# The gate and up biases of 32 experts: rows spread by GpSimd and added by VectorE in place of bias matmuls

## The chip, the cores and the metric

The kernel runs on one core of one Trainium2 chip. The metric is the device time of one execution in microseconds (us). Before the change the median of three runs is 2063.8 us (2061.73 to 2067.09).

## What is computed

One layer of an encoder: a mixer, cross-attention and a mixture of experts over 1024 tokens of width 1024, all in float32. The change lies in the experts. Each token goes to 4 of 32 experts; an expert multiplies its tokens by a gate/up matrix of 1024x2048, adds a bias of 2048, puts the halves through a clamped SwiGLU and multiplies by a down matrix of 1024x1024. Cut to that:

```python
def expert_block(args):
    xb, e = args
    gu = xb @ w_gate_up[e] + b_gate_up[e]
    gate = jnp.minimum(gu[:, :D_EXPERT], SWIGLU_LIMIT)
    up = jnp.clip(gu[:, D_EXPERT:], -SWIGLU_LIMIT, SWIGLU_LIMIT)
    glu = gate * jax.nn.sigmoid(SWIGLU_ALPHA * gate)
    return ((up + 1.0) * glu) @ w_down[e] + b_down[e]
```

`SWIGLU_LIMIT` is 7, `SWIGLU_ALPHA` 1.702.

## The kernel before, in words

**Order of the experts.** Up to the first expert the kernel computes the mixer, the attention and the router, and fills a table of slots: which token, with which weight, stands at which place of which expert. Expert 31 (`STATIC`) comes first, since it needs no ranking. The others are ranked by their number of tokens while the first one runs, and the ranking is written to `ordr`, from which the number of each next expert is read (`prologue`, L925). The first 17 ranks (`N32`) have a remainder of up to 32 tokens beyond 128: they are called heavy here. The 14 others have up to 128 tokens: light. `rank_order` mixes heavy and light ones. What exceeds these sizes is left to a loop at the end (`beyond`).

**One expert.** Its weights come in 12 chunks of 1 MB: `j` = 0 to 7 gate and up (two column halves `c`, two halves `g` of the contraction, `t` for gate or up), 8 to 11 down. Float32 is multiplied as a sum of products of rounded parts: each chunk `raw` is split into `eh` by ScalarE (L134) and the rest `el` by VectorE (L135), and `main_mm` (L1038) runs three matmuls for each of its four slices (L1062, L1063, L1064). An expert has 24 places, two per chunk, and the work of the other engines is issued at a place: `glu_main` for half 0 at place 7 and for half 1 at 15, then `h_main` (transposes of `hh`, L1009, and the split into `hthl`), `x_main` of the next expert, and at 23 `y_main`, which scatters the result into `acc_d` by GpSimd. The tables `PLACE_*` say where the transposes stand, `AHEAD_*` how many chunks ahead the splits run at each place. The order of the instructions on each engine is that of the code.

**Remainders.** The up to 32 rows of a heavy expert go through plain float32 matmuls in `rem_mm` (L1085), sixteen per chunk pair, at places that `plan` puts into `agenda`. Their bias is added in `h_rem` from a small tile `bT`, transposed; the change doesn't touch it.

**The bias.** `b_gate_up` has 2048 values per expert. `bias_load` and `bias_table` bring all of it into one tile `BT` before the first expert: gate halves on partitions 0 to 63, up halves on 64 to 127, each as a rounded part (32 partitions) and a rest (32). In `main_mm`, at the first gate chunk of each half, a pair of matmuls (L1049, in a loop over `t`) picks the expert's row by a one-hot column of `ohr` and writes it to all 128 rows of the banks for gate and up; the products of the chunks are summed on top (`start=j >= 8 and ...`). `ohr` comes from the ranking (`ranks`). `glu` then reads the banks: two clamps from PSUM on VectorE (L1000, L1002), the sigmoid on ScalarE (L1001), two products on VectorE (L1003, L1004).

**Queues.** SP issues the loads of the chunks (L973) and of the small index tables `idx` and `idr`; a chunk is asked for when a buffer is free (`load_more`). GpSimd issues the gathers of token rows (L936, `xg` and `xgr`, for the next expert) and the scatters (L940), and the first expert's chunks from the third on. Pool `s8` has 20 tiles of a chunk's size ([128, 2048]), `s4` 7 of [128, 1024], `t2` 6 of [128, 512].

Of the kernel before, what the change touches and what calls it, by code (L numbers as in the profile page):

```python
# [9 lines left out]
F32 = mybir.dt.float32  # L10
F32R = mybir.dt.float32r
# [52 lines left out]
def rem_rows(r):  # L64
    if r < N64 or r == STATIC:
        return 64
    return 32 if r < N32 else 0
# [12 lines left out]
def kernel(ctx: ExitStack, tc: tile.TileContext, A, out, dbg=None):  # L80
    nc = tc.nc
    PS = bass.MemoryType.PSUM
    cp = ctx.enter_context(tc.tile_pool(name="cp", bufs=1))
    dp = ctx.enter_context(tc.tile_pool(name="dp", bufs=1, space=bass.MemoryType.DRAM))
# [7 lines left out]
    def mm_bank(name="mm"):  # L92
        return mmp.tile([P, H2], F32, name=name, tag="mm")
# [7 lines left out]
    def s8(name, shape, dt=F32):  # L101
        return mp.tile(list(shape), dt, name=name, tag="s8", bufs=20)

    def s4(name, shape, dt=F32):
        return mp.tile(list(shape), dt, name=name, tag="s4", bufs=7)

    def t2(name, shape=(P, H2), dt=F32):
        return mp.tile(list(shape), dt, name=name, tag="t2", bufs=6)

    def small(name, shape, dt=F32, bufs=1):  # L110
        return mp.tile(list(shape), dt, name=name, bufs=bufs)
# [5 lines left out]
    def f(ap):  # L117
        return ap.bitcast(F32)
# [81 lines left out]
    acc_d = dp.tile([S + P, D], F32, name="acc_d")  # L200
    h_d = dp.tile([S + P, D], F32, name="h_d")
    x1_d = dp.tile([2, KT, P, H2], F32, name="x1_d")
    tab_d = dp.tile([NE * ESTR, 2], I32, name="tab_d")
    ov_d = dp.tile([NBLK, 2], I32, name="ov_d")
    hs = [slice(h * H2, (h + 1) * H2) for h in range(2)]
# [64 lines left out]
    eid = cp.tile([P, 8], F32, name="eid")  # L270
# [66 lines left out]
    b = sum_cols([sx])  # L337
# [13 lines left out]
    b = sum_cols([sx])  # L351
# [226 lines left out]
    ps = {}  # L578
# [38 lines left out]
    for ft in range(KT):  # L617
        wh, wl = next_w(0)
        for h in range(2):
            xr = t2("xres")  # L620
            nc.sync.dma_start(out=xr, in_=A["xT"][h, ft])
            for g, (yh, yl) in enumerate(((ych, ycl), (yfh, yfl))):
                ps = mm_bank()
# [117 lines left out]
    for fc in range(2):  # L741
        VW.append([(s8(f"vwh{fc}{q}", [P, 4, H2], F32R), s8(f"vwl{fc}{q}", [P, 4, H2], F32R)) for q in range(2)])
        for hd in range(4):
            w = next_w(0)
            for mt in range(2):
                ps = mm_bank()
# [3 lines left out]
                j = hd * 2 + mt  # L750
# [45 lines left out]
    scat = []  # L796
    tiles = [dict() for _ in range(8)]
    lt = {}
    BT = []

    def tile_r(x2):

# [114 lines left out]
    order = rank_order()  # L917
    ready, ex = [False], []
    st = [None] * NE
# [78 lines left out]
    def glu(hdst, pg, pu, n, m, tmp=None):  # L998
        g, sg, u = tmp or (t2("g"), t2("sg"), t2("u"))
        nc.vector.tensor_scalar(g[:m, :n], pg, LIMIT, None, op0=ALU.min)  # L1000
        nc.scalar.activation(sg[:m, :n], g[:m, :n], AF.Sigmoid, scale=ALPHA)  # L1001
        nc.vector.tensor_scalar(u[:m, :n], pu, LIMIT, -LIMIT, op0=ALU.min, op1=ALU.max)  # L1002
        nc.vector.tensor_tensor(g[:m, :n], g[:m, :n], sg[:m, :n], op=ALU.mult)  # L1003
        nc.vector.scalar_tensor_tensor(hdst, u[:m, :n], 1.0, g[:m, :n], op0=ALU.add, op1=ALU.mult)  # L1004
# [33 lines left out]
    def main_mm(i, j, middle=None):  # L1038
        s = st[i]
        c, g, t = (j // 4, (j % 4) // 2, j % 2) if j < 8 else (j % 2, (j - 8) // 2, 0)  # L1040
        key, l = ("gu"[t] + str(c), s["xt"]) if j < 8 else ("d" + str(c), s["ht"])
        if g == 0 and j >= 8:
            s[key] = mm_bank(key)
        elif g == 0 and t == 0:
            r = s["r"]
            for t in range(2):
                tsl = slice(t * 64, t * 64 + 64)
                b = s["gu"[t] + str(c)] = mm_bank(key)
                nc.tensor.matmul(b, ohr[tsl, r:r + 1].to_broadcast([64, P]), BT[0][tsl, hs[c]], start=True, stop=False)  # L1049
        raw, wh, wl = ch[12 * i + j][:3]  # L1050
        ps = s[key]
        if wh is None:
            for k in range(4):
                nc.tensor.matmul(ps, f(l[:, 0, g * 4 + k, :]), raw[:, k, :], start=j >= 8 and g == 0 and k == 0, stop=g == 1 and k == 3)  # L1054
                if k % 2 and steps:
                    steps.pop(0)()
                if k == 1 and middle:
                    middle()
            return
        for k in range(4):  # L1060
            kk = g * 4 + k
            nc.tensor.matmul(ps, l[:, 0, kk, :], wh[:, k, :], start=j >= 8 and g == 0 and k == 0, stop=False)  # L1062
            nc.tensor.matmul(ps, l[:, 0, kk, :], wl[:, k, :], start=False, stop=False)  # L1063
            nc.tensor.matmul(ps, l[:, 1, kk, :], wh[:, k, :], start=False, stop=g == 1 and k == 3)  # L1064
            if k % 2 and steps:
                steps.pop(0)()
            if k == 1 and middle:
                middle()
# [21 lines left out]
    def glu_main(i, c):  # L1090
        s = st[i]
        s[f"h{c}"] = t2("hh")
        glu(s[f"h{c}"], s[f"g{c}"], s[f"u{c}"], H2, P)

    def h_main(i, c):
        s = st[i]
# [8 lines left out]
    def h_rem(i, c):  # L1105
# [15 lines left out]
        nc.vector.tensor_scalar(g, tv[:, :, 0], LIMIT, None, op0=ALU.min)  # L1121
        nc.scalar.activation(sg, g, AF.Sigmoid, scale=ALPHA)
        nc.vector.tensor_scalar(u, tv[:, :, 1], LIMIT, -LIMIT, op0=ALU.min, op1=ALU.max)
# [75 lines left out]
    def plan(i):  # L1199

        lead, lx, lt, l0, l1, ly = REM
        at = lambda p, fn, *arg: agenda.setdefault(p, []).append(lambda: fn(*arg))
# [7 lines left out]
        at(p + 22 + ly, y_rem, i)  # L1210

    agenda = {}
    for i in range(1, NE):
        if rem_rows(order[i]):
            plan(i)


# [8 lines left out]
        ex.append(e)  # L1226

    def bias_load():

        BT.extend([s4("BT", [P, D], F32R), s8("braw", [P, D])])  # L1230
        for i in range(4):
            nc.scalar.dma_start(out=BT[1][i * 32:(i + 1) * 32], in_=A["b_gate_up"][:, (i // 2) * D:(i // 2 + 1) * D])

    def bias_table():
        nc.scalar.activation(BT[0], BT[1], AF.Copy)
        for i in (32, 96):
            nc.vector.tensor_tensor(BT[0][i:i + 32], BT[1][i:i + 32], f(BT[0][i:i + 32]), op=ALU.subtract)

    def x2_chunk(c0, hooks):
        h, cn = c0 // H2, HF  # L1240
# [31 lines left out]
    xA = x2_chunk(0, places([(load_router,)], [(load_bias,)], [(row_table,)], [(padding,)], [(prepare,)], [(prepare_bias,)]))  # L1272
    xB = x2_chunk(HF, places(*two_tiles(0, xA, 0)))
    C = two_tiles(2, xB, HF)
    C[5].append((bias_load,))
    xC = x2_chunk(H2, places(*C))
    prologue(0)
    first = lambda: load_more(RAWS_FIRST)
# [8 lines left out]
        [(tile_s, 5), (tile_e, 5)]))  # L1287
    dump("h", h_d)
    dump("acc", acc_d)
    ohr = small("ohr", [P, NE], F32R)  # L1290
    ordr = small("ordr", [1, NE + 1], I32)

    nc.vector.tensor_copy(ohr[:, STATIC:STATIC + 1], eid[:, 4:5])
    x_main(0, 0)
    tile_r(xD)
    bias_table()
    x_main(0, 1)
    tile_a(6, xD, H2 + HF)
    tile_a(7, xD, H2 + HF)
# [5 lines left out]
    def count_order():  # L1305
        rk = s4("rk", [P, D])
        cnt, key, gt, R = rk[:, 0:4], rk[:, 32:64], rk[:, 64:96], rk[:, 96:128]
# [20 lines left out]
        def ranks():  # L1328
            ps = sm_bank("ordps")
            nc.tensor.matmul(ps[:1, 0:NE], eid[:32, 0:1], R[:32], start=True, stop=True)  # L1330
            nc.vector.tensor_copy(ordr[:, 0:NE], ps[:1, 0:NE])
            nc.vector.tensor_copy(ohr, R)
            ready[0] = True

        ps3 = {}
# [171 lines left out]
    def both(*fs):  # L1507
        def go():
            for g in fs:
# [6 lines left out]
    base, r = fin["base"], fin["r"]  # L1516
# [4 lines left out]
                                 in_=base, in_offset=None)  # L1521
# [84 lines left out]
```

## Time and profile before

| | |
|---|---|
| median of three runs | 2063.8 us (2061.73 to 2067.09) |
| profiled execution, its own time | 2069.46 us |
| its span | 2067.6 us |
| PE busy | 2028.4 us, 98% |
| PE weight loads busy | 1513.3 us, 73% |
| VectorE busy | 1585.7 us, 77% |
| ScalarE busy | 1122.3 us, 54% |
| GpSimd busy | 227.3 us, 11% |
| DMA | 513.26 MB, mean 248 GB/s |

The profile is one execution, taken by the hardware profiler. PE is TensorE's matmuls, PEld its weight loads (they overlap the matmuls), DVE VectorE, ACT ScalarE, POOL GpSimd, SP the engine that issues most loads. An engine's busy time is the union of its instructions. Matmuls are pipelined: the length given for one is longer than the distance from it to the next. "L1064" is line 1064 of the kernel. The granted clock of TensorE over the span was 0.99 of full speed, the higher of its two levels, 2.4 GHz.

### The profile page before, as it was taken

Reading aid. Unit: us, or ns where it says so; the run is one execution under the profiler, and the core shown is the slowest. Engines: PE = TensorE matmul, PEld = TensorE weight load, DVE = VectorE, ACT = ScalarE, POOL = GpSimd, SP = SyncE. Lnnn points to the kernel's source line nnn. Section 1 sums busy time; section 2 is a strip of 40 time slices with the busy share of each in tenths; the row PEclk is TensorE's granted clock in tenths of the full one; section 3 lists DMA queues with packets and bytes.
Section 4 is the critical chain, followed back from the end, with each engine's and each line's share of the span. In section 5 each row is a group of like instructions: output and inputs, shape, how many; then the busy total and the mean of one; then the engine's idle time right before and its main releaser. Section 6 shows DMA issues by size and latency. Waiting matters only on the chain. (4 is left out here: it accounts for less than half of the span.)

```text
span 2067.6 us, 28604 instructions
## 1 busy us (share of the span) xinstructions
PE 2028.4 (98%) x10745; PEld 1513.3 (73%) x10745; DVE 1585.7 (77%) x1991; ACT 1122.3 (54%) x1195; POOL 227.3 (11%) x190
## 2 busy tenths in 40 slices
PE   8999999999999999999999999999999999999996
PEld 6888988888984567677776677676776676776764
DVE  6667668445576788888888798888988788888876
ACT  5233533334213566675666676666666576666754
POOL 0000100000133111010101111010111110110101
PEclk9999999999999999999999999999999999999999
DMA  4112434112358689898897998898998799898976
GB/s 156 47 62 72 133 125 161 31 42 86 107 192 302 231 286 358 302 318 321 310 363 254 333 320 323 306 362 302 318 327 304 283 339 320 306 348 298 332 301 249
DMA packets 104640, 513.26 MB, mean 248 GB/s; under 512 B 21298, under 2 KB 25651, under 8 KB 55347
## 3 DMA queue, kind: packets, MB, share of 16 engines
q1 hardware_dynamic: 83600, 445.87, 57.3%
q0 software_dynamic: 14080, 48.54, 9.4%
q10 hardware_dynamic: 6818, 16.99, 2.3%
q8 instruction: 86, 1.41, 0.3%
q14 instruction: 56, 0.45, 0.1%
HBM read 473.41 MB, written 37.95 MB: 247 GB/s over the span
## 5 line engine op out<-in xcount | busy, mean ns | idle before, releaser
L135 DVE TENSOR_TENSOR el<-raw,eh 128x2048 fp32r<-128x2048 f32 x372 | 831.0, 2287 | 121.3 <-ACT eh L134 119.8
L134 ACT ACTIVATE eh<-raw 128x2048 fp32r<-128x2048 f32 x372 | 690.6, 1908 | 7.1 <-PEq L1402 4.6
L1062 PE MATMUL g<-eh,xthl 128*128 128x512 f32 x992 | 401.2, 404 | 0.0
L1064 PE MATMUL g<-eh,xthl 128*128 128x512 f32 x992 | 388.1, 391 | 2.2 <-issue 2.2
L1063 PE MATMUL g<-el,xthl 128*128 128x512 f32 x992 | 388.5, 392 | 1.3 <-DVE el L135 1.3
L1062 PEld LDWEIGHTS g<-eh,xthl 128*128 128x128 f32 x992 | 186.5, 188 | 79.3 <-issue 39.7
L1064 PEld LDWEIGHTS g<-eh,xthl 128*128 128x128 f32 x992 | 186.6, 188 | 43.6 <-issue 2.6
L1063 PEld LDWEIGHTS g<-el,xthl 128*128 128x128 f32 x992 | 186.8, 188 | 36.9 <-DVE el L135 1.6
L1062 PE MATMUL d<-eh,hthl 128*128 128x512 f32 x496 | 205.9, 415 | 0.0
L1064 PE MATMUL d<-eh,hthl 128*128 128x512 f32 x496 | 195.1, 393 | 0.0
L1063 PE MATMUL d<-el,hthl 128*128 128x512 f32 x496 | 194.0, 391 | 0.0
L1085 PE MATMUL r<-raw,xrt 128*32 128x512 f32 (+1 forms) x1152 | 144.8, 598 | 0.7 <-ACT xrt L1036 0.7
L1001 ACT ACTIVATE sg<-g 128x512 f32<-128x512 f32 x64 | 40.4, 631 | 175.8 <-DVE g L1000 172.3
L940 POOL DMA_INDIRECT acc_d<-y,idx x31 | 74.4, 2400 | 393.1 <-ACT y L1131 296.4
L1062 PEld LDWEIGHTS d<-eh,hthl 128*128 128x128 f32 x496 | 93.2, 188 | 28.1 <-ACT xthl L134 10.9
L1064 PEld LDWEIGHTS d<-eh,hthl 128*128 128x128 f32 x496 | 93.1, 188 | 21.2
L1063 PEld LDWEIGHTS d<-el,hthl 128*128 128x128 f32 x496 | 93.6, 189 | 16.0
L134 ACT ACTIVATE hthl<-tp 128x512 fp32r<-128x512 f32 x62 | 37.1, 599 | 120.5 <-PE tp L1009 120.5
L145 PE MATMUL mm<-xh,wh 128*128 128x512 f32 x232 | 92.2, 397 | 6.0 <-ACT xh L137 6.0
L147 PE MATMUL mm<-xh,wl 128*128 128x512 f32 x232 | 91.0, 392 | 0.5 <-DVE wl L135 0.5
L146 PE MATMUL mm<-xl,wh 128*128 128x512 f32 x232 | 91.2, 393 | 0.0
L135 DVE TENSOR_TENSOR wl<-wraw,wh 128x1024 fp32r<-128x1024 f32 (+1 forms) x57 | 70.3, 1233 | 22.9 <-ACT wh L134 18.9
(377 smaller groups left out, 3243.0 us busy)
## 6 DMA issues: line engine op xcount, KB each, us to landing
raw<-in_w_exp SPq DMA_DIRECT2D x375, 1024.0 KB
raw<-in_w_exp POOLq DMA_DIRECT2D x9, 1024.0 KB
wraw<-in_w_in SPq DMA_DIRECT2D x15, 512.0 KB
xraw<-in_xT SPq DMA_DIRECT2D x16, 256.0 KB
wraw<-in_w_k SPq DMA_DIRECT2D x8, 512.0 KB
wraw<-in_w_v SPq DMA_DIRECT2D x8, 512.0 KB
wraw<-in_w_out SPq DMA_DIRECT2D x8, 512.0 KB
xres<-in_xT SPq DMA_DIRECT2D x16, 256.0 KB
```

What stands on the lines that cost most here:

```text
L134: nc.scalar.activation(dh, src, AF.Copy)
L135: nc.vector.tensor_tensor(dl, src, f(dh), op=ALU.subtract)
L145: nc.tensor.matmul(ps, lh, rh, start=start and i == 0, stop=False)
L146: nc.tensor.matmul(ps, lh, rl, start=False, stop=False)
L147: nc.tensor.matmul(ps, ll, rh, start=False, stop=stop and i == n - 1)
L940: nc.gpsimd.indirect_dma_start(out=dst, out_offset=bass.IndirectOffsetOnAxis(ap=idx, axis=0), in_=src, in_offset=None, compute_op=ALU.add)
L1001: nc.scalar.activation(sg[:m, :n], g[:m, :n], AF.Sigmoid, scale=ALPHA)
L1062: nc.tensor.matmul(ps, l[:, 0, kk, :], wh[:, k, :], start=j >= 8 and g == 0 and k == 0, stop=False)
L1063: nc.tensor.matmul(ps, l[:, 0, kk, :], wl[:, k, :], start=False, stop=False)
L1064: nc.tensor.matmul(ps, l[:, 1, kk, :], wh[:, k, :], start=False, stop=g == 1 and k == 3)
L1085: nc.tensor.matmul(ps[o:o + m], lhs[:, g * 4 + kk, :], ch[12 * i + j - 1 + t][0][:, kk, :], start=k == 0 and g == 0, stop=k == 4 // n - 1 ...
```

## The change

Both halves of the banks are now started by the chunks' own products, and the bias is added when VectorE reads them. For each expert and half, `bias_row` loads one row of 4 KB (512 gate and 512 up values) into partition 0 of a tile `bt` [128, 2, 512] by SP's queue, and `bias_rows` copies partition 0 to all 128 partitions by GpSimd (`partition_broadcast`). `glu_main` reads the banks with an add of `bt`, and no longer uses `glu`. The one of `(up + 1.0)` is added once to the table of biases (`bias_one`), which goes to DRAM as `bias_d`; the clamp of up is from -6 to 8 accordingly. The sigmoid is taken of the unclamped gate and clamped afterwards by its value at 7 (`SIGMOID_LIMIT`). `BIAS` holds the places: the row of half 0 is asked for three places before the expert's start and copied at its place 1, that of half 1 at places 5 and 9; in the first expert the first row comes before `x_main(0, 0)`. `BT`, `ohr`, `bias_table` and the pairs of matmuls are gone. `glu` stays for the loop `beyond`.

```diff
+BIAS = ((-3, 1), (5, 9))
...
-        if g == 0 and j >= 8:
+        if g == 0:
             s[key] = mm_bank(key)
-        elif g == 0 and t == 0:
-            r = s["r"]
-            for t in range(2):
-                tsl = slice(t * 64, t * 64 + 64)
-                b = s["gu"[t] + str(c)] = mm_bank(key)
-                nc.tensor.matmul(b, ohr[tsl, r:r + 1].to_broadcast([64, P]), BT[0][tsl, hs[c]], start=True, stop=False)
...
-            nc.tensor.matmul(ps, l[:, 0, kk, :], wh[:, k, :], start=j >= 8 and g == 0 and k == 0, stop=False)
+            nc.tensor.matmul(ps, l[:, 0, kk, :], wh[:, k, :], start=g == 0 and k == 0, stop=False)
...
         s[f"h{c}"] = t2("hh")
-        glu(s[f"h{c}"], s[f"g{c}"], s[f"u{c}"], H2, P)
+        g, sg, u = t2("g"), t2("sg"), t2("u")
+        bt = s[f"b{c}"]
+        nc.vector.tensor_tensor(g, s[f"g{c}"], bt[:, 0, :], op=ALU.add)
+        nc.scalar.activation(sg, g, AF.Sigmoid, scale=ALPHA)
+        nc.vector.tensor_tensor(u, s[f"u{c}"], bt[:, 1, :], op=ALU.add)
+        nc.vector.tensor_scalar(u, u, LIMIT + 1.0, 1.0 - LIMIT, op0=ALU.min, op1=ALU.max)
+        nc.vector.scalar_tensor_tensor(u, sg, SIGMOID_LIMIT, u, op0=ALU.min, op1=ALU.mult)
+        nc.vector.scalar_tensor_tensor(s[f"h{c}"], g, LIMIT, u, op0=ALU.min, op1=ALU.mult)
+
+    def bias_row(i, c):
+
+        s = st[i]
+        bt = s[f"b{c}"] = s4("bt", [P, 2, H2])
+        nc.sync.dma_start(out=bt[0:1], in_=bias_d[ds(s["e"], 1)].rearrange("o (t c f) -> o t c f", t=2, c=2)[:, :, c, :])
+
+    def bias_rows(i, c):
+        bt = st[i][f"b{c}"]
+        nc.gpsimd.partition_broadcast(bt.rearrange("p t f -> p (t f)"), bt[0:1].rearrange("p t f -> p (t f)"))
...
-    for i in range(1, NE):
-        if rem_rows(order[i]):
+    for i in range(NE):
+        for c, (row, rows) in enumerate(BIAS):
+            if i or c:
+                agenda.setdefault(24 * i + row, []).append(lambda i=i, c=c: bias_row(i, c))
+            agenda.setdefault(24 * i + max(rows, 0 if i else 1), []).append(lambda i=i, c=c: bias_rows(i, c))
+        if i and rem_rows(order[i]):
             plan(i)
...
-    def bias_table():
-        nc.scalar.activation(BT[0], BT[1], AF.Copy)
-        for i in (32, 96):
-            nc.vector.tensor_tensor(BT[0][i:i + 32], BT[1][i:i + 32], f(BT[0][i:i + 32]), op=ALU.subtract)
+        bb.append(s8("braw", [NE, 2 * D]))
+        nc.scalar.dma_start(out=bb[0], in_=A["b_gate_up"])
+
+    def bias_one():
+
+        nc.vector.tensor_scalar(bb[0][:, D:], bb[0][:, D:], 1.0, None, op0=ALU.add)
+        nc.scalar.dma_start(out=bias_d[:, :], in_=bb[0])
```

**GpSimd, a light expert and the heavy one behind it.** The rows are the engine's instructions in their order; `acc_d<-y` is the scatter of an expert's result, `xg` and `xgr` are gathers for the next expert, `acc_d<-yr` scatters a remainder. Before:

```order
L940 DMA acc_d<-y,idx 1152x1024
L936 DMA xg<-h_d,idx 128x1024
L936 DMA xgr<-h_d,idr 32x1024
L940 DMA acc_d<-y,idx 1152x1024
L936 DMA xg<-h_d,idx 128x1024
L940 DMA acc_d<-yr,ids 2304x512
L940 DMA acc_d<-y,idx 1152x1024
```

Now, with the lines of the changed kernel:

```order
L943 DMA acc_d<-y,idx 1152x1024
L1107 ISA bt<-bt 128x1024
L939 DMA xg<-h_d,idx 128x1024
L939 DMA xgr<-h_d,idr 32x1024
L1107 ISA bt<-bt 128x1024
L943 DMA acc_d<-y,idx 1152x1024
L1107 ISA bt<-bt 128x1024 x2
L939 DMA xg<-h_d,idx 128x1024
L943 DMA acc_d<-yr,ids 2304x512
L943 DMA acc_d<-y,idx 1152x1024
```

In the light expert the first copy stands behind the scatter of the expert before and ahead of both gathers, the second behind the gathers; in the heavy expert both copies stand between the scatter and the gather `xg`.

**GpSimd, the first expert.** `tab_d` is the table of slots, `rk` a scratch tile of the ranking, `raw` the first expert's chunks. Before:

```order
L901 DMA tab_d<-pl,slot 36864x2
L906 MEMSET spacer 1x4
L1312 IOTA rk 32x64
L936 DMA xgr<-h_d,idr 64x1024
L973 DMA raw<-in_w_exp 128x2048 x3
```

Now:

```order
L904 DMA tab_d<-pl,slot 36864x2
L909 MEMSET spacer 1x4
L1327 ISA
L1327 IOTA rk 32x64
L1107 ISA
L1107 ISA bt<-bt 128x1024
L939 DMA xgr<-h_d,idr 64x1024
L976 DMA raw<-in_w_exp 128x2048 x3
```

Three instructions came between the scatters into the table and the gather `xgr`: a copy, and two rows without tiles, one ahead of the iota and one ahead of the copy. Two more such rows stand ahead of the program's first copy (L1107) and ahead of the last tensor_tensors (L1507).

**VectorE, the second half of a light expert's products.** `el` is the rest of a chunk's split, `g_...` and `u_...` are the banks in PSUM. Before:

```order
L135 TENSOR_TENSOR el<-raw,eh 128x2048 x6
L1000 TENSOR_SCALAR g<-g_7759 128x512
L1002 TENSOR_SCALAR u<-g_7761 128x512
L1003 TENSOR_TENSOR g<-g,sg 128x512
L1004 SCALAR_TENSOR_TENSOR hh<-u,g 128x512
L135 TENSOR_TENSOR el<-raw,eh 128x2048 x2
L135 TENSOR_TENSOR hthl<-tp,hthl 128x512
```

Now:

```order
L137 TENSOR_TENSOR el<-raw,eh 128x2048 x6
L1092 TENSOR_TENSOR g<-g_7774,bt 128x512
L1094 TENSOR_TENSOR u<-u_7794,bt 128x512
L1095 TENSOR_SCALAR u<-u 128x512
L1096 SCALAR_TENSOR_TENSOR u<-sg,u 128x512
L1097 SCALAR_TENSOR_TENSOR hh<-g,u 128x512
L137 TENSOR_TENSOR el<-raw,eh 128x2048 x2
L137 TENSOR_TENSOR hthl<-tp,hthl 128x512
```

Four operations between the splits became five; the splits stand as before. On TensorE nothing moved but the 128 bias matmuls, which are gone.

## Rows read from the trace of the kernel before

**Rows 1.** Busy time by stretch: us, PE, PEld, DVE, ACT, POOL, PEclk, DMA share, GB/s.

```profile
1240.22:1325.92 85.70, 85.70 (x444) 61.24 (x440) 73.25 (x64) 56.21 (x47) 11.34 (x6) 1.00 0.89 320
```

**Rows 2.** Groups by line, shapes apart: busy us, mean ns of one, idle before.

```profile
L1049 PE MATMUL g<-BT,ohr 64*128 64x512 f32 x128 | 32.3, 501 | 0.0
```

**Rows 3.** PE in order of time, around a pair behind the stream: start, busy us.

```profile
1284.45 0.39 PE L1064 MATMUL g<-eh,xthl 128*128 128x512 f32 x1
...
1285.54 0.39 PE L1063 MATMUL g<-el,xthl 128*128 128x512 f32 x1
1285.77 0.40 PE L1064 MATMUL g<-eh,xthl 128*128 128x512 f32 x1
```

**Rows 4.** PE in order of time, behind two remainders, a pair behind the first.

```profile
1224.25 1.92 PE L1085 MATMUL r<-raw,xrt 128*32 128x512 f32 x16
...
1226.87 0.39 PE L1063 MATMUL g<-el,xthl 128*128 128x512 f32 x1
...
1232.20 1.92 PE L1085 MATMUL r<-raw,xrt 128*32 128x512 f32 x16
...
1234.40 0.40 PE L1063 MATMUL g<-el,xthl 128*128 128x512 f32 x1
```

**Rows 5.** Groups of VectorE, shapes apart: the clamps of the remainders.

```profile
L1121 DVE TENSOR_SCALAR ga<-re 128x128 f32<-128x128 f32 x34 | 7.7, 227 | 1.2
...
L1121 DVE TENSOR_SCALAR ga<-re 128x256 f32<-128x256 f32 x2 | 0.6, 294 | 0.1
```

**Rows 6.** A light expert: VectorE, then GpSimd, then the transposes of hh.

```profile
1273.41 13.30 DVE L135 TENSOR_TENSOR el<-raw,eh 128x2048 fp32r<-128x2048 f32 x6 [1.11 <-ACT eh L134]
1286.63 0.69 DVE L1000 TENSOR_SCALAR g<-g 128x512 f32<-128x512 f32 x1
...
1288.74 0.69 DVE L1004 SCALAR_TENSOR_TENSOR hh<-u,g 128x512 f32<-128x512 f32 x1
1289.82 4.49 DVE L135 TENSOR_TENSOR el<-raw,eh 128x2048 fp32r<-128x2048 f32 x2 [0.39 <-ACT eh L134]
1294.85 0.69 DVE L135 TENSOR_TENSOR hthl<-tp,hthl 128x512 fp32r<-128x512 f32 x1 [0.54 <-ACT hthl L134]
...
1279.12 2.45 POOL L940 DMA_INDIRECT acc_d<-y,idx  x1 [6.45 <-ACT y L1131]
...
1289.89 2.98 POOL L936 DMA_INDIRECT xgr<-h_d,idr  x1 [0.30 <-issue]
...
1300.79 0.60 PE L1009 MATMUL tp<-cst,hh 128*128 128x128 f32 x4
```

**Rows 7.** GpSimd: an iota (by line: busy us, mean ns), the last tensor_tensors (by time).

```profile
L763 POOL IOTA ptab<- 128x288 int32 x1 | 0.4, 388 | 221.4 <-DVE vtl L135 221.4
...
2045.79 4.70 POOL L1493 TENSOR_TENSOR fa<-fa,gfin 128x1024 f32<-128x1024 f32 x2 [16.23 <-ACT fa L1492]
```

**Rows 8.** GpSimd and VectorE in order of time, early in the kernel.

```profile
245.62 4.02 POOL L198 TENSOR_TENSOR row<-row,sq 128x512 f32<-128x512 f32 x2 [7.76 <-ACT sq L197]
...
246.17 2.32 DVE L135 TENSOR_TENSOR wl<-wraw,wh 128x1024 fp32r<-128x1024 f32 x1
...
249.61 1.23 DVE L135 TENSOR_TENSOR wl<-wraw,wh 128x1024 fp32r<-128x1024 f32 x1 [0.34 <-ACT wh L134]
```

**Rows 9.** A heavy expert: the last product of its second half and the transposes.

```profile
1257.78 0.69 DVE L1004 SCALAR_TENSOR_TENSOR hh<-u,g 128x512 f32<-128x512 f32 x1
...
1261.44 0.60 PE L1009 MATMUL tp<-cst,hh 128*128 128x128 f32 x4
```

**Rows 10.** The first expert: gathers on GpSimd and the transposes that use them.

```profile
611.89 0.99 POOL L936 DMA_INDIRECT xg<-h_d,idx  x1 [5.40 <-DMA xres<-x_d]
...
617.68 0.63 PE L1009 MATMUL tp<-cst,xg 128*128 128x128 f32 x4 [1.42 <-DMA xg<-h_d,idx]
...
651.25 0.93 POOL L936 DMA_INDIRECT xgr<-h_d,idr  x1 [3.88 <-ACT hthl L134]
...
659.35 0.71 PE L1035 MATMUL tp<-cst,xgr 64*128 64x64 f32 x8
```

More of the change, by code (lines that the diff above doesn't have):

```diff
@@ L30 @@
 ALPHA = 1.702
+SIGMOID_LIMIT = float(1.0 / (1.0 + np.exp(-ALPHA * LIMIT)))
 N64 = 0
@@ L202 @@
     x1_d = dp.tile([2, KT, P, H2], F32, name="x1_d")
+    bias_d = dp.tile([NE, 2 * D], F32, name="bias_d")
     tab_d = dp.tile([NE * ESTR, 2], I32, name="tab_d")
@@ L798 @@
     lt = {}
-    BT = []
+    bb = []
     def tile_r(x2):
@@ L1053, in main_mm @@
             for k in range(4):
-                nc.tensor.matmul(ps, f(l[:, 0, g * 4 + k, :]), raw[:, k, :], start=j >= 8 and g == 0 and k == 0, stop=g == 1 and k == 3)
+                nc.tensor.matmul(ps, f(l[:, 0, g * 4 + k, :]), raw[:, k, :], start=g == 0 and k == 0, stop=g == 1 and k == 3)
                 if k % 2 and steps:
@@ L1228, in bias_load @@
     def bias_load():
-        BT.extend([s4("BT", [P, D], F32R), s8("braw", [P, D])])
-        for i in range(4):
-            nc.scalar.dma_start(out=BT[1][i * 32:(i + 1) * 32], in_=A["b_gate_up"][:, (i // 2) * D:(i // 2 + 1) * D])
-    def bias_table():
-        nc.scalar.activation(BT[0], BT[1], AF.Copy)
-        for i in (32, 96):
-            nc.vector.tensor_tensor(BT[0][i:i + 32], BT[1][i:i + 32], f(BT[0][i:i + 32]), op=ALU.subtract)
+        bb.append(s8("braw", [NE, 2 * D]))
[3 more added lines that the diff above has]
+        nc.scalar.dma_start(out=bias_d[:, :], in_=bb[0])
     def x2_chunk(c0, hooks):
@@ L1274 @@
     C = two_tiles(2, xB, HF)
-    C[5].append((bias_load,))
+    C[1].append((bias_load,))
+    C[5].append((bias_one,))
     xC = x2_chunk(H2, places(*C))
@@ L1289 @@
     dump("acc", acc_d)
-    ohr = small("ohr", [P, NE], F32R)
     ordr = small("ordr", [1, NE + 1], I32)
-    nc.vector.tensor_copy(ohr[:, STATIC:STATIC + 1], eid[:, 4:5])
+    bias_row(0, 0)
     x_main(0, 0)
     tile_r(xD)
-    bias_table()
     x_main(0, 1)
@@ L1331, in ranks @@
             nc.vector.tensor_copy(ordr[:, 0:NE], ps[:1, 0:NE])
-            nc.vector.tensor_copy(ohr, R)
             ready[0] = True
```

## The prediction

> **What bounds the kernel now.** I read the busy time by stretch first. One period of the expert loop, a light and a heavy expert, lasts 85.70 us, and TensorE is busy in all of it, VectorE in 73.25 [rows 1]; the loop is TensorE's, VectorE has 12.4 us of air, and no other engine comes near. Then the groups by line: the bias is added by 128 matmuls [rows 2], two at a time on the two halves of the array, so 64 pairs. The reader should see in the listing of TensorE what a pair costs there, which is not its own length.
>
> **What the removal gives.** In the stream one matmul follows the other by 0.23 us. Around a pair, L1064 at 1284.45 to the second matmul behind the pair at 1285.54 is 1.09 us, where two steps of 0.23 would stand: a pair costs 0.63 [rows 3]. Behind a remainder's sixteen matmuls it is 1224.25 to 1226.87 with a pair and 1232.20 to 1234.40 without: 0.42 [rows 4]. 27 pairs stand behind the stream and 18 behind transposes (taken at the first price), 17 behind remainders and 2 in the first expert (taken at the second): 45 x 0.63 + 19 x 0.42 = **36.3 us**, all of it on the engine that is never idle. The table's cast and subtractions before the first expert go too; I take nothing for them, since the router's work shares that stretch.
>
> **What VectorE gets.** Four operations become five per half. The two reads of PSUM stay (an add instead of a minimum), two multiplications with clamps take the place of two, and the clamp of u is new, from SBUF to SBUF. It is in no row of before; the nearest clamps take 227 ns for 128 columns and 294 for 256 [rows 5], 0.52 ns a column, so 0.43 us for 512 by the same line; the old clamp of this size, 0.69 [rows 6], is the upper bound. The chain from g to hh took from 1286.63 to 1288.74 + 0.69, 2.8 us [rows 6]; it becomes 3.2. VectorE alone pays 4 x 0.43 = 1.7 us a period out of 12.4: hidden, if nothing else comes.
>
> **What GpSimd gets.** 64 copies of a row of 1,024 values to 128 partitions. Bounds for one: 0.39 us, an iota that writes 288 columns, and 2.35, a tensor_tensor that reads two tensors of 1,024 (4.70 for two) [rows 7]. By columns the iota would be 1.38 with its fixed part scaled too; the copy does no arithmetic and reads one row, so it is nearest to the iota: I take **X = 1.2 us**. GpSimd has the time. Who pays is VectorE: a subtraction of 1.23 us took 2.32 when it met a GpSimd tensor_tensor that had begun 0.55 us before, and GpSimd's next one was stretched in turn, 4.02 us for two [rows 8]. One of them stands still while the other runs. The 12 subtractions `el` of each expert are of that kind, with two inputs in SBUF. The Trainium skill (SBUF — State Buffer, Who interferes with whom) says that a VectorE instruction with two SBUF inputs contends with a GpSimd instruction that reads SBUF, and not with one that only writes; the first case agrees with the row, and the second is a rival below.
>
> So each copy that meets an `el` costs VectorE X. Does that reach TensorE? Take a **light expert** [rows 6]. The first copy stands behind the scatter of y, which ends at 1281.57, inside six `el` that run to 1286.71: they, and all behind them, come X later. The next two end at 1289.82 + 4.49 + 1.2 = 1295.51. The second copy stands behind the gather xgr, that ends at 1292.87: it meets the second of these two. If it waits, the rows are there at 1296.7 and glu starts; if it goes ahead, the `el` ends at 1296.7 and the split hthl (0.6) comes first, 1297.3. With 3.2 us for the chain hh is ready at 1299.9 to 1300.5. TensorE wants it at 1300.79 less two pairs of 0.63 = 1299.53: late by 0.4 to 1.0, I take 0.7. In a **heavy expert** the first copy meets the six `el` likewise, the second falls into the remainder's small operations; hh, ready at 1258.47 before [rows 9], comes X + 0.4 + 0.4 later, 1260.47, and is wanted at 1261.44 - 1.05 = 1260.39: late by 0.1. For other X: 2X - 1.7 and X - 1.1. There are 13 light and 17 heavy experts of this pattern: 13 x 0.7 + 17 x 0.1 = **10.8 us lost**.
>
> **The first expert.** The order of GpSimd shows three new instructions without tiles ahead of a copy or an iota in the first expert, and a fourth ahead of the last tensor_tensors: I read them as swaps of the engine's set of instructions. The fourth falls into 16.23 us of idle time [rows 7]. The first falls into idle time too. The other two stand with a copy between the last scatter of the table and the gather xgr at 651.25, which had 3.88 us of idle time before it [rows 10]. A swap's price is in no row; it lies between nothing and the way of a load from issue to use, 611.89 to 617.68, 5.8 us [rows 10]; I take 5, near the upper end, since code must come as that data does. The gather is 2 x 5 + 1.2 - 3.88 = 7.3 us late. At 5.8 us to use it was there at 657.05 for transposes at 659.35: 2.3 us of slack, and TensorE arrives two pairs (0.84) earlier, so it stops 7.3 - 2.3 + 0.84 = **5.8 us** (0 to 7.5 by the bounds). The Trainium skill (GPSIMD Engine Reference, Instruction dispatch) gives about 6 us for the first call to freshly loaded code, not visible as an instruction; no row here shows one, and by it these 5.8 us would be 7.8 and the time 2046.
>
> **Hidden.** Each row comes by one small load on SP's queue, between loads of 1 MB that wait for TensorE to free buffers; the row is asked for four places ahead of the copy, and the copy six ahead of its use. ScalarE's sigmoid reads g as before.
>
> **Sum.** 36.3 - 10.8 - 5.8 = 19.7 us less. The profiled execution took 2069.46 us, 5.7 over the median of the three runs, 2063.8; the difference is taken from the median: **2044 us**, and by X from 1.0 to 1.5 us 2037 to 2057.
>
> **Rivals.**
> - *No lock* (chance 0.27): the copy counts as a writer, or it reads its row so fast that `el` hardly waits. For it: it reads 4 KB of one partition, not a tensor. Against it: [rows 8]. Only the first expert costs: 36.3 - 5.8 = 30.5, 2033 us.
> - *Both copies meet in heavy experts too* (0.17): the second row lands later than I think, and its copy falls among the four `el` ahead of glu. Each heavy expert then loses 2X - 1.1 = 1.3 us, 22.1 in place of 1.7: 36.3 - 9.1 - 22.1 - 5.8 = -0.7: 2064 us, no change.
> - *Slower: VectorE becomes the bound* (0.14): a copy takes as long as a tensor_tensor, X = 2.35. VectorE then has 73.25 + 4 x (0.43 + 2.35) = 84.4 us a period of some 83.4, and the tables of how far ahead to split no longer cover it. Light experts lose 3.0, heavy 1.25: 60 us against 30.5 of gain, 2094 us. It decides from X = 1.66, where 13 x (2X - 1.7) + 17 x (X - 1.1) = 30.5. Against it: the copy does less than a tensor_tensor.
>
> **How the numbers follow.** The forecast has a chance of 0.42. Range for 8 in 10: from 2027, where neither a lock nor a swap costs anything (2063.8 - 36.3), to 2068, a little over the case without change; outside lies the slower rival. 0.3% is 6 us. Faster by more: 0.42 + 0.27 = 0.69; within: 0.17; slower: 0.14.
>
> **What would show it.** No rows of BT's matmuls, and steps of 0.23 where pairs stood. Copies of about 1.2 us on GpSimd, longer where they wait; `el`, 2.25 us now (4.49 for two), stretched by X once or twice per expert. Waits of TensorE's hh transposes on VectorE in light experts, 0.4 to 1.0 us, and none in heavy ones. One wait of 5 to 6 us on the gather xgr in the first expert, near 659. I am wrong if `el` never stretches (then near 2033), if X is over 1.6, or if VectorE waits for rows that have not landed.

## The result: slower, near the rival that was given least

The changed kernel takes 2091.1 us (median of four, 2088.5 to 2093.6) where the kernel before, run beside it, takes 2064.6: a ratio of 1.0129 (1.0108 to 1.0149), 26.5 us slower. The forecast was 2044 us, with a range up to 2068. The profiled execution of the change took 2089.2 us.

The page of the changed kernel, and the groups by line of the operations that matter (busy us, mean ns of one, idle before):

```profile
span 2087.4 us, 28925 instructions
...
PE 2003.3 (96%) x10617; PEld 1497.7 (72%) x10617; DVE 1655.9 (79%) x2052; ACT 1113.4 (53%) x1194; POOL 356.3 (17%) x254
...
L137 DVE TENSOR_TENSOR el<-raw,eh 128x2048 fp32r<-128x2048 f32 x372 | 872.3, 2399 | 116.4 <-ACT eh L136 116.4
...
L1107 POOL PARTITION_BROADCAST bt<-bt x64 | 140.6, 2197 | 157.5 <-DMA bt<-bias_d 126.5
```

The same subtractions on the page of the kernel before:

```profile
L135 DVE TENSOR_TENSOR el<-raw,eh 128x2048 fp32r<-128x2048 f32 x372 | 831.0, 2287 | 121.3 <-ACT eh L134 119.8
```

TensorE is busy 25 us less than before (2028.4), but it stands still for 84 us where it stood for 39. The 372 subtractions `el` take 872.3 us, against 831.0: in the trace 43 of them take about 3.25 us, and nearly all others 2.29, as before. A copy takes 2.20 us on average.

Where TensorE stands still, by the listing of its waits (us in total, times, longest):

```profile
PE d L1061 <- DVE hthl L137: 13.9, 13, 1.5
PE tp L1012 <- DVE fr L1475: 9.8, 1, 9.8
PE tp L1012 <- DVE hh L1097: 9.0, 14, 0.7
PE tp L1038 <- DMA xgr<-h_d,idr: 7.1, 2, 6.8
PE u L1059 <- DVEq L1416: 6.1, 1, 6.1
```

Two kinds stand here. Two rows repeat from expert to expert, for `hthl` and for `hh`. Three are single events of 6 to 10 us: the gather `xgr` (6.8 of its 7.1) in the first expert, the branch into the loop `beyond` (L1416), and the last expert (the row names `fr`, the last thing VectorE did before; the data that was late is `hh`).

**The loop came out even.** One period of a light and a heavy expert, columns as in [rows 1]:

```profile
1267.71:1353.81 86.10, 84.23 (x433) 60.33 (x433) 78.23 (x68) 55.62 (x47) 18.03 (x10) 1.00 0.88 316
```

86.10 us against 85.70 [rows 1]. TensorE has 1.9 us of gaps in it, and VectorE is busy 5.0 us longer, where the prediction had 1.7 for the fifth operation and up to some 4.8 for the copies. From the transposes of the first expert's second `hh` to those 57 halves on, in the thirtieth expert, it was 1265.07 us before and is 1263.81 now.

**What a meeting looks like.** In order of time, first a heavy expert, then the light one behind it:

```profile
1233.25 15.23 DVE L137 TENSOR_TENSOR el<-raw,eh 128x2048 fp32r<-128x2048 f32 x6 [0.66 <-ACT eh L136]
...
1233.55 3.15 POOL L1107 PARTITION_BROADCAST bt<-bt  x1
...
1244.52 1.96 POOL L1107 PARTITION_BROADCAST bt<-bt  x1 [7.81 <-DMA bt<-bias_d]
...
1267.71 0.63 PE L1012 MATMUL tp<-cst,hh 128*128 128x128 f32 x4 [0.71 <-DVE hh L1097]
...
1280.24 14.27 DVE L137 TENSOR_TENSOR el<-raw,eh 128x2048 fp32r<-128x2048 f32 x6 [1.11 <-ACT eh L136]
...
1287.88 2.42 POOL L1107 PARTITION_BROADCAST bt<-bt  x1
...
1295.74 0.43 DVE L1095 TENSOR_SCALAR u<-u 128x512 f32<-128x512 f32 x1
...
1296.62 1.51 POOL L1107 PARTITION_BROADCAST bt<-bt  x1
...
1297.00 1.53 DVE L1097 SCALAR_TENSOR_TENSOR hh<-g,u 128x512 f32<-128x512 f32 x1
...
1302.86 0.68 DVE L137 TENSOR_TENSOR hthl<-tp,hthl 128x512 fp32r<-128x512 f32 x1
...
1303.59 0.50 PE L1061 MATMUL d<-eh,hthl 128*128 128x512 f32 x1 [1.06 <-DVE hthl L137]
```

Six `el` took 13.30 us before [rows 6]. With one copy among them they take 14.27, with two 15.23: 0.97 us per meeting. In the light expert the second copy meets the last product of the first half, 1.53 us instead of 0.69. And TensorE waits in both: 0.71 us for `hh` in the heavy expert, 1.06 for `hthl` in the light one. A wait costs 0.16 us more than its gap, since the gap is counted from the end of the last matmul, 0.39 long, where the next would have begun 0.23 after its start [rows 3]. Set beside the same matmuls of e1 (below; it makes no copies from the second expert on), TensorE falls behind by 0.87 us at 1267.71, by 0.25 at the transposes of `hh` at 1298.68 and by 1.22 at 1303.59, so 1.47 in the light expert.

The two engines take turns. The first two of the six `el` at 1233.25, by themselves:

```profile
1233.25 2.29 DVE L137 TENSOR_TENSOR el<-raw,eh 128x2048 fp32r<-128x2048 f32 x1 [0.66 <-ACT eh L136]
...
1235.46 3.24 DVE L137 TENSOR_TENSOR el<-raw,eh 128x2048 fp32r<-128x2048 f32 x1
```

The subtraction that runs when the copy is issued (1233.55) keeps its 2.29 us and ends at 1235.54. The copy ends 1.16 us after that, at 1236.70. The next subtraction, issued at 1235.46, ends 2.00 us after the copy. In the trace 55 of the 64 copies end 1.16 us after the VectorE operation that they met, whenever they were issued: the copy's 3.15 us are a wait and then its own time, and so are the subtraction's 3.24.

**The first expert**, GpSimd in order of time, then the transposes that wait for its gather, then TensorE behind that wait by the view of stretches:

```profile
626.38 1.30 POOL L1107 PARTITION_BROADCAST bt<-bt  x1 [9.54 <-issue]
...
648.86 0.18 POOL L1327 IOTA rk<- 32x64 f32 x1 [7.41 <-DMA idr<-tab_d]
...
657.75 1.30 POOL L1107 PARTITION_BROADCAST bt<-bt  x1 [8.71 <-issue]
659.25 1.13 POOL L939 DMA_INDIRECT xgr<-h_d,idr  x1 [0.20 <-issue]
...
664.18 1.09 PE L1038 MATMUL tp<-cst,xgr 64*128 64x64 f32 x8 [6.79 <-DMA xgr<-h_d,idr]
```

```profile
664.00:670.00 6.00, 4.81 (x18) 2.17 (x20) 0.00 (x0) 0.60 (x1) 0.63 (x1) 0.50 1.01 426
```

Under the lines of the iota and of the copy the trace also has these instructions of GpSimd's sequencer (durations in ns, first and last start in us):

```profile
L1327 POOLq MODIFY_POOL_CONFIG  x2: 18/18/18, 641.5 to 641.5; - x2
...
L1107 POOLq MODIFY_POOL_CONFIG  x4: 1/16/32, 616.9 to 649.3; - x4
```

GpSimd stands still for 7.41 and 8.71 us ahead of the iota and of the copy, the two places with an instruction without tiles. There the trace shows a pair of instructions that change GpSimd's configuration, at 641.5 and at 649.3, and the engine's next operation starts 7.3 and 8.5 us behind them. The gather starts at 659.25, 8.0 us later than before [rows 10], though the work around it runs earlier. After the wait TensorE's granted clock is 0.50 for the next stretch, its lower level (1.2 GHz).

**The last expert**, the chain that ended last:

```profile
2041.90 0.35 SPq L976
2042.51 12.76 DMA bt<-bias_d
2055.45 1.30 POOL bt L1107
2056.81 0.57 issue
```

The row of 4 KB was asked for behind the four loads of the final stage and one of a chunk, 1 MB each, and landed 12.8 us later. TensorE's wait for the last `hh`, 9.84 us here, was 1.93 before:

```profile
2041.34 0.63 PE L1009 MATMUL tp<-cst,hh 128*128 128x128 f32 x4 [1.93 <-DVE fr L1461]
```

**The branch**, all engines in order of time:

```profile
1975.26 2.28 DVE L137 TENSOR_TENSOR el<-raw,eh 128x2048 fp32r<-128x2048 f32 x1
1977.92 1.91 ACT L136 ACTIVATE eh<-raw 128x2048 fp32r<-128x2048 f32 x1 [4.47 <-DVEq L1416]
...
1978.12 0.79 PE L1059 MATMUL u<-eh,xthl 128*128 128x512 f32 x1 [6.08 <-DVEq L1416]
```

TensorE's first matmul into the bank for up goes on when VectorE has ended its third `el` and passed its own branch at L1416. Before, the first matmul into that bank was the bias pair, ahead of the branch; TensorE's wait near here was 2.16 us then, put down to no other engine:

```profile
1972.12 0.50 PE L1064 MATMUL g<-eh,xthl 128*128 128x512 f32 x1 [2.16 <-issue]
```

### The profile page after: what moved, and what is told of

It is laid out like the page before. It is cut to its first block, busy times and chain, and to the rows that moved or that the text cites. A ratio compares the mean times of both kernels' runs of the same rounds, so it can differ in the third digit from the quotient of the medians.

```text
span 2087.4 us, 28925 instructions
## 1 busy us (share of the span) xinstructions
PE 2003.3 (96%) x10617; PEld 1497.7 (72%) x10617; DVE 1655.9 (79%) x2052; ACT 1113.4 (53%) x1194; POOL 356.3 (17%) x254
## 5 line engine op out<-in xcount | busy, mean ns | idle before, releaser
L137 DVE TENSOR_TENSOR el<-raw,eh 128x2048 fp32r<-128x2048 f32 x372 | 872.3, 2399 | 116.4 <-ACT eh L136 116.4
L1059 PE MATMUL u<-eh,xthl 128*128 128x512 f32 x496 | 196.7, 396 | 6.1 <-DVEq L1416 6.1
L1059 PE MATMUL g<-eh,xthl 128*128 128x512 f32 x496 | 201.5, 406 | 0.2 <-ACT xthl L136 0.2
L1060 PE MATMUL g<-el,xthl 128*128 128x512 f32 x496 | 195.0, 393 | 1.3 <-DVE el L137 1.3
L1061 PE MATMUL g<-eh,xthl 128*128 128x512 f32 x496 | 193.9, 391 | 0.5 <-DVE xthl L137 0.5
L1060 PE MATMUL u<-el,xthl 128*128 128x512 f32 x496 | 193.6, 390 | 0.0
L1061 PE MATMUL u<-eh,xthl 128*128 128x512 f32 x496 | 193.6, 390 | 0.0
L1107 POOL PARTITION_BROADCAST bt<-bt x64 | 140.6, 2197 | 157.5 <-DMA bt<-bias_d 126.5
L1059 PEld LDWEIGHTS g<-eh,xthl 128*128 128x128 f32 x496 | 93.1, 188 | 61.3 <-issue 38.6
L1059 PEld LDWEIGHTS u<-eh,xthl 128*128 128x128 f32 x496 | 93.6, 189 | 25.0 <-issue 6.5
L1061 PEld LDWEIGHTS g<-eh,xthl 128*128 128x128 f32 x496 | 93.2, 188 | 21.9 <-DVE xthl L137 1.3
L1061 PEld LDWEIGHTS u<-eh,xthl 128*128 128x128 f32 x496 | 93.4, 188 | 19.7
L1060 PEld LDWEIGHTS u<-el,xthl 128*128 128x128 f32 x496 | 93.7, 189 | 18.3
```

The source lines that it names most:

```text
L137: nc.vector.tensor_tensor(dl, src, f(dh), op=ALU.subtract)
L1059: nc.tensor.matmul(ps, l[:, 0, kk, :], wh[:, k, :], start=g == 0 and k == 0, stop=False)
L1107: nc.gpsimd.partition_broadcast(bt.rearrange("p t f -> p (t f)"), bt[0:1].rearrange("p t f -> p (t f)"))
```

## The experiments

The kernel before ran beside them; times are compared by their ratio to it.

**e1: one pair of tiles for all experts** (the other experts' biases are left out).

```diff
-        for c, (row, rows) in enumerate(BIAS):
+        for c, (row, rows) in enumerate(BIAS if i == 0 else ()):
...
-        bt = s[f"b{c}"]
+        bt = st[0][f"b{c}"]
```

> All experts add the two bias tiles of the first expert: from the second expert on there are no row loads and no copies, and the other 31 experts' biases are left out. The five VectorE operations per half stay. Theory (the copies slow VectorE's subtractions, and that makes the loop's waits): the loop's waits of TensorE for hh and hthl go, some 34 us, the wait ahead of the loop beyond shrinks by 3, the last expert's wait of 8 us goes: near 2045 us. Rival (the fifth VectorE operation and the longer chain alone use up VectorE's air): the waits in the loop stay, only the last expert's goes: near 2083.

2052.4 us, ratio 0.995 (0.9934 to 0.9965). A period of its loop:

```profile
1255.69:1339.02 83.33, 83.33 (x434) 60.63 (x432) 74.70 (x69) 55.85 (x47) 8.68 (x6) 1.00 0.90 332
```

No gap is left: 83.33 us, with all five VectorE operations in place. The same 57 halves take 1231.4 us. So the loop's waits came with the copies, 1263.8 - 1231.4 = 32.4 us of them. The time is 7 us above the theory's: the loop gave 32.4 us where 34 was expected, the branch 1.1 (6.1 to 5.0) where 3 was, the last expert 6.1 (9.8 to 3.7) where 8 was, and about 2 us stay open. The 6.6 us for `xgr` stayed, as this kernel keeps the first expert's swaps.

**e2: the row of half 1 asked for earlier.**

```diff
-BIAS = ((-3, 1), (5, 9))
+BIAS = ((-3, 1), (-2, 9))
...
-                agenda.setdefault(24 * i + row, []).append(lambda i=i, c=c: bias_row(i, c))
+                agenda.setdefault(24 * i + (row if i else max(row, 5)), []).append(lambda i=i, c=c: bias_row(i, c))
```

> The row of each half 1 is asked for at place -2 instead of 5 (its copy stays at place 9), in the first expert as before. Theory: the last expert's copy no longer waits behind the loads of the final stage, 8 us less; in heavy experts the second copy runs at its place and no longer among the subtractions ahead of glu, which gives back up to 17 x 1.06 = 18 us: 2065 us. Rival (a copy meets some subtraction wherever it runs): only the 8 us of the last expert, 2083.

2085.6 us, ratio 1.0105 (1.0076 to 1.0134). The wait in the last expert fell from 9.8 to 1.7 us. In the loop nothing was won: 14.6 us of waits for `hthl` and 9.3 for `hh`. GpSimd no longer waits for rows, and its copies take still longer:

```profile
L1107 POOL PARTITION_BROADCAST bt<-bt x64 | 161.7, 2562 | 19.5 <-issue 19.0
```

The rival was right, with 2083 us: a copy that doesn't wait for its row runs at once behind the first one and meets the same subtractions.

**e3: the iota at the start.**

```diff
-        nc.gpsimd.iota(iob, pattern=[[1, NBLK]], base=0, channel_multiplier=0, allow_small_or_imprecise_dtypes=True)
...
+        nc.gpsimd.iota(iob, pattern=[[1, NBLK]], base=0, channel_multiplier=0, allow_small_or_imprecise_dtypes=True)
         nc.gpsimd.iota(tokid, pattern=[[P, 8]], base=P, channel_multiplier=1)
```

> The iota of the ranking is made at the start of the kernel, in a tile of its own, so that GpSimd keeps one set of instructions through the first expert. Theory (each swap of sets costs GpSimd 7 to 9 us there and makes the gather xgr late): the two swaps in the first expert go, the wait of 6.8 us ahead of the xgr transposes and the low clock behind it too: 9 to 12 us less, 2080. Rival (the gather waits for its index table, not for GpSimd): no change, 2091.

2077.3 us, ratio 1.0068 (1.0044 to 1.0091): 1.0129 - 1.0068 is 0.6%, some 13 us less than the change. The traces agree: from the transposes of the first expert's first `hh` to those of its second it is 28.6 us before, 39.7 in the change and 28.9 here. The two gaps of GpSimd are gone and `xgr` is there in time:

```profile
644.67 1.30 POOL L1109 PARTITION_BROADCAST bt<-bt  x1
...
648.51 0.96 POOL L941 DMA_INDIRECT xgr<-h_d,idr  x1 [2.54 <-DMA idr<-tab_d]
```

The instructions that change GpSimd's configuration at 641.5 and 649.3 are gone with them, and the rival, that the gather waits for its index table, is out. So the instructions without tiles are swaps of what GpSimd can run, and two of them in the first expert cost 11 us by the traces and some 13 by the times. It is about half of what the change lost.

**e4: the load writes all partitions.**

```diff
-        nc.sync.dma_start(out=bt[0:1], in_=bias_d[ds(s["e"], 1)].rearrange("o (t c f) -> o t c f", t=2, c=2)[:, :, c, :])
+        nc.sync.dma_start(out=bt, in_=bias_d[ds(s["e"], 1)].rearrange("o (t c f) -> o t c f", t=2, c=2)[:, :, c, :].to_broadcast([P, 2, H2]))
...
-            agenda.setdefault(24 * i + max(rows, 0 if i else 1), []).append(lambda i=i, c=c: bias_rows(i, c))
```

> No copies: the row's load itself writes all 128 partitions (512 KB instead of 4 KB, 33 MB more in all), on SP's queue at the places of the row loads. Theory: without copies no collisions and no swaps, 36 + 12 us back, and the transfers hide beside a DMA share of 0.89: near 2040 us, the last expert's wait of 8 us staying. Rival (the loop becomes the DMA's): 2 MB more per period at the loop's rate is 6 us of DMA time on 76, at or over the length of the period; the splits wait for chunks and the time stays at 2060 to 2090.

2048.3 us, ratio 0.994 (0.9912 to 0.9968): faster than the kernel before. It is 8 us above the theory's number. Five waits for `xgr` (7.3 us together, 2.1 the longest) are new; that they come from the row loads of 512 KB beside the gather is likely, not shown. The last expert's wait is 10.6 us.

**e5 and e6: copies that nobody reads, and memsets in their place.** e5 is the change with the adds reading the first expert's tiles; in e6 GpSimd writes the tiles by a memset from the second expert on (both leave out the other experts' biases).

```diff
-        bt = s[f"b{c}"]
+        bt = st[0][f"b{c}"]
...
+        if i:
+            nc.gpsimd.memset(bt.rearrange("p t f -> p (t f)"), 0.0)
+            return
```

> As the kernel with one pair of bias tiles (2052.4 us), but the row loads and the copies of all experts run again where the change has them; nobody reads them, and the adds take the first expert's tiles (the other experts' biases are left out). Theory (the copies slow VectorE by meeting its subtractions, whoever reads them): TensorE's waits for hh and hthl are back and the subtractions are as long as in the change, 2.40 us on average; 2052 + 34 = 2086 us at most, less the last expert's wait that needs a reader (8 us): 2078 to 2086. Rival (VectorE loses its time by waiting for the copies' arrival): near 2052.

> As the kernel with unread copies, but from the second expert on GpSimd writes each tile of 128 x 1024 by a memset instead of copying the row, at the same places: it writes as much and reads nothing. Theory by the first rival of the prediction turned round (the collision needs GpSimd to read while VectorE reads two tensors): the subtractions fall back to 2.25 to 2.29 us, the loop's waits go, near 2052 us. Rival (writing is enough): subtractions and waits as with copies, 2078 to 2086.

e5: ratio 1.0127 (1.0101 to 1.0153), as slow as the change; e6: 0.9955 (0.9939 to 0.9971), as fast as e1. A period of e5:

```profile
1273.74:1359.78 86.04, 84.19 (x433) 60.31 (x433) 78.23 (x68) 55.62 (x47) 17.63 (x10) 1.00 0.90 322
```

A period of e6, and its groups:

```profile
1257.25:1340.58 83.33, 83.33 (x433) 60.63 (x432) 74.77 (x69) 55.89 (x47) 13.16 (x10) 1.00 0.90 331
...
L137 DVE TENSOR_TENSOR el<-raw,eh 128x2048 fp32r<-128x2048 f32 x372 | 830.6, 2287 | 122.1 <-ACT eh L136 122.1
...
L1108 POOL MEMSET bt<- 128x1024 f32 x62 | 78.0, 1258 | 167.5 <-DMA bt<-bias_d 167.2 <-issue 0.3
```

VectorE is busy 78.23 us a period with four copies and 74.77 with four memsets that write as much: 0.87 us per copy. No one reads the tiles in either, so it isn't the arrival of the rows; and a memset leaves the subtractions at 2287 ns, as before, none of them over 2.3 us. Writing the tile, then, is not what VectorE waits for; what is left is that the copy reads. The Trainium skill (SBUF — State Buffer, Who interferes with whom) gives VectorE's second pair of ports as shared with GpSimd, and contention for it to a VectorE instruction with two SBUF inputs against a GpSimd instruction that reads; e5 and e6 agree with it on both sides. A copy and a memset are different instructions in other ways too, and no run here changes the reading alone.

e5's time is above the 2078 to 2086 expected, by ratio some 2090; its loop is that of the change. Its wait in the last expert fell from 9.8 to 2.4 us, as expected, but the time from there to the end, 27.2 us in the change, is 33.2: the last copy waits for its row as long as in the change (14.8 and 14.4 us), and now the fourth swap behind it is no longer hidden.

```profile
2061.41 1.44 POOL L1107 PARTITION_BROADCAST bt<-bt  x1 [14.78 <-DMA bt<-bias_d]
2069.58 6.69 POOL L1507 TENSOR_TENSOR fa<-fa,gfin 128x1024 f32<-128x1024 f32 x2 [6.74 <-issue]
```

**e7, e8 and e9: the rows by broadcasting loads, with their places mended.** e7 is e4 with both rows of the last expert at place -3; e8 moves the rows to -7 and 1 (the last expert's second stays at -3, the first expert's at 5); e9 also puts the loop `beyond` one chunk later.

```diff
-                agenda.setdefault(24 * i + row, []).append(lambda i=i, c=c: bias_row(i, c))
+                agenda.setdefault(24 * i + (row if i < NE - 1 else -3), []).append(lambda i=i, c=c: bias_row(i, c))
```

```diff
-BIAS = ((-3, 1), (5, 9))
+BIAS = ((-7, 1), (1, 9))
```

```diff
-BEYOND = 1
+BEYOND = 2
```

> As the kernel whose row loads write all 128 partitions (2048.3 us), with both rows of the last expert asked for at place -3. Theory: the last expert's wait of 10.6 us (1.9 before) goes: 2039 to 2041. Rival (the row's 512 KB lands no sooner, since the final stage's loads take the engines): 2048.

> As the one before, with the rows of the loop asked for at places -7 and 1 instead of -3 and 5. Theory (the five waits for xgr, 7.3 us, come from row loads that run beside the gather and its tables): the waits go, 5 to 7 us below the kernel before it. Rival (the DMA engines are full in the loop, and what is moved meets something else): the same or slower.

> As the kernel with 128-partition row loads at places -7 and 1, with the loop beyond one chunk later (BEYOND = 2), so that the first matmul into the bank for up stands ahead of the loop's branch. Theory (without the bias pair that first matmul is behind the branch and waits until VectorE, with three subtractions still ahead of it, passes its own branch): the wait of 5.0 us there falls to the 2.2 of before, 3 us less: ratio 0.988. Rival (the wait is that of the branch itself, wherever it stands): no change, the wait stays at 5 us.

e7: ratio 0.991 (0.988 to 0.994), some 2045 us where 2039 to 2041 was expected; the last expert's wait is 2.0 us, against 10.6 in e4. e8: 0.9892 (0.9874 to 0.991); the waits for `xgr` are 4.6 us, the longest 1.1, where e7 has 3.1, 1.4 and e4 7.3, 2.1. The two ratios overlap, and 5 to 7 us were expected: whether the places helped is not shown. e9: 0.9879 (0.9862 to 0.9895), 2038.9 us, 25 us faster than the kernel before and the best of those that leave nothing out. The longest waits of TensorE in e9:

```profile
PE mm L147 <- ACT xh L139: 5.9, 1, 5.9
PE posps L884 <- DVE w L865: 2.6, 2, 1.3
PE cntps L1330 <- DVE rk L1325: 2.3, 1, 2.3
...
PE tp L1127 <- DVE u L1095: 2.2, 1, 2.2
```

The first three lie ahead of the loop. The wait of the bank for up behind the branch, 5.0 us in e8, is gone; the fourth row, 2.2 us, is what stands just behind the branch now, as expected. The difference in time, 0.0013, is within the intervals, so the trace shows it and the times don't. A period:

```profile
1200.00:1283.33 83.33, 83.33 (x434) 60.63 (x433) 74.77 (x69) 55.85 (x47) 9.78 (x6) 1.00 0.96 359
```

The DMA share is 0.96, against 0.89 [rows 1], and TensorE still has no gap.

**e10: the change with copies, its three single places mended** (the edits of e3, of e7 and of e9).

> As the change, copies and all, with three places mended: the iota made at the start, the last expert's second row asked for at place -3, and BEYOND = 2. Theory (the loop comes out even, since what the bias pairs gave is lost to the copies' collisions, and the 27 us over before lie in the first expert, at the branch and in the last expert): 13 + 8 + 3 us less than the change, ratio to before 1.000 to 1.003. Rival (the loop itself is slower than before, and the three places are not additive): a ratio of 1.005 or more.

Ratio 1.0007 (0.9993 to 1.0021). The theory's sum holds: what the change lost against the kernel before lies in the first expert, at the branch and in the last expert, and the loop with its copies is worth nothing either way (its 57 halves take 1264.1 us here). The three are shown together; of each alone only the first expert's is clear of noise in the times (e3), the other two stand on the waits in the traces.

**e11: no bias at all.**

```diff
-        elif g == 0 and t == 0:
-            r = s["r"]
-            for t in range(2):
-                tsl = slice(t * 64, t * 64 + 64)
-                b = s["gu"[t] + str(c)] = mm_bank(key)
-                nc.tensor.matmul(b, ohr[tsl, r:r + 1].to_broadcast([64, P]), BT[0][tsl, hs[c]], start=True, stop=False)
```

> The kernel before without the 128 bias matmuls and nothing in their place: the gate and up biases of all tokens but the remainders are left out. Theory (a pair costs TensorE 0.63 or 0.42 us, all of it on the path): 36 us less, less up to 3 at the branch: ratio 0.983 to 0.985. Rival (part of the pairs' time hid waits of TensorE for VectorE, which now show): ratio 0.987 or more.

Ratio 0.9848 (0.9831 to 0.9866): 31.4 us. A period:

```profile
1246.71:1330.04 83.33, 83.33 (x434) 60.63 (x432) 73.23 (x64) 55.87 (x47) 10.57 (x6) 1.00 0.89 331
```

85.70 - 83.33 = 2.37 us for the four pairs of a period. The branch takes some back: 5.0 us of wait there, as in e1. The fifth VectorE operation is not in this kernel, and its period is that of e1 and e9: the operation is hidden.

## Why the prediction was wrong, step by step

- **What the removal gives: right.** The loop gains 2.37 us per period without biases (e11), and 1265.1 - 1231.4 = 33.7 us over the 57 halves with the fifth operation (e1). 36.3 was given for all 64, so 32.3 for 57.
- **The fifth operation: right.** 0.43 us as estimated, hidden.
- **X: right.** A copy that meets nothing takes 1.30 us; 1.2 was taken. The slower rival's reason, a copy as long as a tensor_tensor, is wrong, though the mean of 2.20 looks like it: the rest is its wait for the subtraction that runs (1.96 to 3.15 us in the heavy expert's rows above).
- **"So each copy that meets an `el` costs VectorE X": nearly right**, 0.97 us instead of 1.2. "One of them stands still while the other runs" is what the rows show: the copy waits out one subtraction, and the next subtraction waits out the copy.
- **What of it reaches TensorE, 10.8 us: this failed**; it is 32.4 (e1 against the change). In the *heavy expert* the second copy did not "fall into the remainder's small operations": its row landed late and it met the `el` ahead of glu, as the second rival had it, 1.93 us in all. Even an early row doesn't help (e2). The wait for `hh` moves TensorE by 0.87 there, where 0.1 was given. In the *light expert* I followed the second half's `hh` and overlooked the first half's `hthl`. Before, it was ready at 1294.85 + 0.69 = 1295.54 [rows 6], and TensorE's first matmul with it came at 1297.16 (row below): 1.62 us of slack, plus 0.39 and 0.54 of idle time ahead of those operations. What comes against it is 0.97 (first copy), 0.43 (clamp), 0.84 (second copy on the product) and 1.26 (TensorE earlier by two pairs), 3.50 less 2.55: 0.95 late, measured 1.06. With the 0.16 behind a wait and the 0.25 at `hh` that is 1.47 per light expert instead of 0.7. The listing has 13 waits for `hthl` and 14 for `hh`: 13 x 1.47 + 14 x 0.87 = 31.3, near the 32.4. Set matmul beside matmul with e1 over the 57 halves, TensorE loses 15.3 us at `hthl` and 12.7 at `hh`, and the rest in steps of about 0.1.

TensorE of the kernel before, in order of time:

```profile
1297.16 0.39 PE L1064 MATMUL d<-eh,hthl 128*128 128x512 f32 x1
```

- **The first expert, 5.8 us: the mechanism right, the size off.** The swaps were there and `xgr` was late by them, but GpSimd stood still for 7.41 and 8.71 us where 5 was taken, and taking both away gives 11 us by the traces and some 13 by the times (e3), the clock's lower level behind the wait included. The Trainium skill (GPSIMD Engine Reference, Instruction dispatch) gives about 6 us for a first call to freshly loaded code; the rows here are above it, and they stand.
- **"Hidden": failed, at a cost, in one place.** I wrote that each row is asked for four places ahead; in the last expert the queue holds the final stage's loads ahead of it. It cost 8 us of waiting (9.84 against 1.93). In the heavy expert above a copy also waited 7.81 us for its row, which e2 shows to cost nothing of its own.
- **The branch was not in the prediction.** That a bias pair also opened the banks, and for up ahead of the branch, was plain in the code. It cost 6.08 - 2.16 = 3.9 us of waiting.
- **The sum by the runs:** the loop comes out even; 11 to 13 (e3), 8 and 4 make 23 to 25 of the 26.5 us, and e10, which mends these three, is at 1.0007. The time landed near the slower rival's 2094, but by another way than that: of its 60 us of losses in the loop there were 32, and the rest lay outside of the loop.

## What to carry to other kernels

A small operation on an engine with air is not free if it takes turns with an engine whose results are awaited: ask which operations it will run beside, and follow every result that the other engine owes, not the last one alone. Before taking out an instruction, look at what else it did, as opening a bank ahead of a branch. And of an operation done once per stage, price the first and the last stage by themselves: here they held the whole net loss. A load that writes all partitions did the copies' work without meeting VectorE at all; with the last expert's rows asked for early and the branch moved (e9), it left a ratio of 0.988.

## What was not expected of the hardware

- That a copy and the subtractions take turns was expected, how exactly was not: the copy ends 1.16 us after the subtraction it met, and the next subtraction 2.00 us after the copy, 0.97 later than it would have, with differences of 0.01 us from one meeting to the next. A memset of the same tile, 1.26 us, waits for no subtraction and costs them nothing (e6).
- A swap of what GpSimd can run shows as idle time of 6.7 us (e5, the fourth) to 9.5 us (the change, the first) ahead of the engine's next operation.
- 33 MB more of row loads, at a DMA share of 0.96, left TensorE's period at 83.33 us in e9. It was not free at every place: the 57 halves take 1238.9 us in e4 and 1233.1 in e9, against 1231.4 in e1.
